# Twenty-eight stores of a hybrid encoder layer, moved from the SP queue to ScalarE's queue

## The chip, the cores and the metric

The kernel runs on one core of one Trainium2 chip, as one program in one launch. The metric is the device time of an execution in microseconds (us), the median of several runs. TensorE (PE) multiplies matrices, VectorE (DVE), ScalarE (ACT) and GpSimd (POOL) work on elements, and SyncE (SP) only issues transfers. Each engine takes its own instructions strictly in order and waits for others by semaphores.

## The reference

One layer of a bidirectional encoder, for 512 tokens of width 1024, in float32. Cut to what matters:

```python
u = x @ w_in                                  # z | x,B,C | dt | q | k | v | gate logits
y_ssd = ssd_branch(z, xbc, dt_f, dt_b, ...) @ w_proj_ssd      # chunked scan in both directions
y_att = attention_branch(q, k, v) @ w_proj_attn               # dilated windows, 12 heads
gates = sigmoid(gate_logits + b_gate)
mix = (gates[:, :, 0] * y_ssd + gates[:, :, 1] * y_att) @ w_out
h = layer_norm(alpha * x + mix, ln1_g, ln1_b)
f = square(relu(h @ w_up)) @ w_down
out = layer_norm(alpha * h + f, ln2_g, ln2_b)
```

## The kernel before

Each product is made of three matmuls (helper `mm3`, L124 to L126): both factors are split into a high and a low part in a reduced float32 format. For a weight tile, `Stream` loads the raw tile on SP (`wraw`, L86, three buffers), ScalarE casts the high part (`wh`, L103) and VectorE subtracts to get the low part (`wl`, L104); `wh` and `wl` have two buffers each, so wh72 takes the buffer of wh70 and wraw80 that of wraw77. Numbers count the weight tiles: tiles 60 to 75 are the gate tiles g0 to g15, tiles 76 and on belong to the projection of the scan's output (`ps_pa`).

The program runs in stages: v and dt first, then the state space scan in four groups of eight heads each, mixed on TensorE with the 6 q, 6 k and 16 gate tiles and the other column tiles of `w_in`; then attention, mixed with the projection; then the merge, the first norm and the two matrix products of the channel part. Within a group the heads come in pairs. For each head ScalarE and VectorE build a 128x512 matrix in pieces of 128x128: `U` from two broadcast rows `bc` (L439 on ScalarE, L441 on VectorE, exponential L442), `G1` and `G2` (L444 and L445 on ScalarE), their sum (L446) and product with `U` (L447) on VectorE. When both heads of pair j are there, TensorE makes `ps_y` of that pair (L348); then come `yt` (L350 on VectorE, L351 on GpSimd), `y` (L352 on VectorE) and its square `sq` (L354 on ScalarE). Group 3 has pairs 12 to 15, that is heads 24 to 31. Later `yh` (L542, ScalarE) and `yl` (L543, VectorE) split y0 to y15 for the projection.

The q, k and gate tiles of the middle stage leave the chip's on-chip memory: `evict` reads the sum from PSUM on ScalarE into a staging tile of 256 KB (tag `stage`, two buffers) and stores it to DRAM. The q and k tiles are loaded again by `load_qk` in attention (L558 and L559), the gates in `proj_a` and `proj_b` (L755 and L763).

TensorE's order is written out by hand (`manual_schedule`). On VectorE, ScalarE and SP a scheduler orders the instructions by its own estimates, so it also decides between which rows a store stands. The loads of attention follow on SP behind the raw weight load wraw80, which needs the slot that wl77 frees.

Of the kernel before, what the change touches and what calls it, by code (L numbers as in the profile page):

```python
# [43 lines left out]
def hybrid_layer_kernel(ctx: ExitStack, tc: tile.TileContext, t: dict, out: bass.AP):  # L44
    nc = tc.nc
    act, dve, pool, pe, dma = nc.scalar, nc.vector, nc.gpsimd, nc.tensor, nc.sync
# [15 lines left out]
    dr_qk = dram.tile([12, P, S], F32, name="dr_qk")  # L62
    dr_v = dram.tile([S, 768], F32, name="dr_v")
    dr_gate = dram.tile([16, P, S], F32, name="dr_gate")
# [203 lines left out]
    def conv_silu(ps, ci, dst):  # L268

        w = lambda k: vec[:, V_CW + ci * 5 + k:V_CW + ci * 5 + k + 1]  # L270
        acc = sp.tile([P, S], F32, name=f"acc{ci}", tag="acc", bufs=2)
        act.activation(acc, ps, AF.Identity, bias=vec[:, V_CB + ci:V_CB + ci + 1], scale=w(2))
        for k, (o0, o1, i0, i1) in ((0, (2, S, 0, S - 2)), (1, (1, S, 0, S - 1)), (3, (0, S - 1, 1, S)), (4, (0, S - 2, 2, S))):
            dve.scalar_tensor_tensor(acc[:, o0:o1], ps[:, i0:i1], w(k), acc[:, o0:o1], op0=ALU.mult, op1=ALU.add)
        act.activation(dst, acc, AF.Tanh)
        dve.scalar_tensor_tensor(dst, dst, 1.0, acc, op0=ALU.add, op1=ALU.mult)

    def tile_task(kind, j):

        wh, wl = ws.get()  # L280
        ps = ps_tile("mm", f"ps_{kind}{j}", 3)
        for k in range(0, KT, 2):
            last_mm[0] = mm3(ps, [(wh[:, q * P:(q + 1) * P], wl[:, q * P:(q + 1) * P]) for q in (k, k + 1)], xs_hl[k:k + 2], k == 0, k == KT - 2)
            if k < KT - 2:
                yield QT
        evict(kind, j, ps)
        yield QT

    def evict(kind, j, ps):
        if kind == "x":  # L290
            dst = sp.tile([P, S], F32, name=f"x{j}", tag="x", bufs=8)
            conv_silu(ps, j, dst)
            fm["x", j] = dst
        elif kind in "BC":
            dst = sp.tile([P, S], F32, name=f"{kind}{j}", tag=kind, bufs=2)
            conv_silu(ps, (16 if kind == "B" else 20) + j, dst)
            fm[kind, j] = dst
        elif kind == "z":
            th = ys[j]
            act.activation(th, ps, AF.Tanh, scale=0.5)  # L300
            dve.scalar_tensor_tensor(th, th, 1.0, ps, op0=ALU.add, op1=ALU.mult)
        elif kind == "g":
            st = xp.tile([P, S], F32, name=f"g{j}", tag="stage", bufs=2)
            act.activation(st, ps, AF.Tanh, scale=0.5, bias=vec[:, V_BG + j:V_BG + j + 1])
            dma.dma_start(dr_gate[j], st)
        else:
            st = xp.tile([P, S], F32, name=f"{kind}{j}", tag="stage", bufs=2)
            sc = 0.125 if kind == "q" else 1.0
            if j < 2:
                act.activation(st, ps, AF.Copy, scale=sc)  # L310
            else:
                act.activation(st.rearrange("p (r i) -> p i r", r=4), ps.rearrange("p (i r) -> p i r", r=4), AF.Copy, scale=sc)
            dma.dma_start(dr_qk[{"q": 0, "k": 6}[kind] + j], st)

    last_mm = [None]

# [718 lines left out]
```

## Time and profile before

| | |
|---|---|
| three runs | 1036.61, 1035.73 and 1035.19 us, median 1035.73 |
| the profiled execution | 1036.7 us, its span in the profile 1034.9 us |
| mean granted clock of TensorE | 0.995 |
| median from issue to landing, 256 KB store of a gate tile | 2.0 us |
| the same, 256 KB load of a q or k tile | 4.3 and 4.7 us |
| the same, 512 KB raw weight tile of `w_in` | 3.5 us |
| all DMA | 140.42 MB, 136 GB/s over the span |

The span is the time from the first to the last recorded instruction on the core; starts in the timeline count from its beginning. A busy TensorE says little of its pace, since matmuls overlap; what counts is where it waits, and whether the waiting one is the engine on whose end the whole ends. All transfers before the change go through one queue, SP's.

### The profile page before, as it was taken

What the parts mean: (1) busy time and instruction counts of PE and PEld (TensorE: products, weight loads), DVE (VectorE), ACT (ScalarE), POOL (GpSimd) and SP (SyncE); (2) the same over time, 40 slices, a digit from 0 to 9 for tenths busy, and PEclk for the clock granted to TensorE, in tenths of its full rate; (3) what the DMA queues carried; (4) which work ended last, traced back from release to release, by engine and by line L of the source; (5) the groups of instructions that cost most, each with busy time, mean ns of one, the idle gap of its engine ahead of it and who ended that gap; (6) DMA issues with size and microseconds to landing.
All of it is one profiled execution on the core that took longest, in us unless ns stands there. A gap on an engine that the chain in (4) does not pass through costs nothing.

```text
span 1034.9 us, 13695 instructions
## 1 busy us (share of the span) xinstructions
PE 1018.9 (98%) x5169; PEld 843.6 (82%) x5169; DVE 650.1 (63%) x1009; ACT 511.1 (49%) x1009; POOL 73.5 (7%) x66
## 2 busy tenths in 40 slices
PE   9999999999999999999899999999999999999997
PEld 7888888888888888888678787898888888888886
DVE  4296978689979897874886276844442334443346
ACT  4444877478758865984564334224332213433120
POOL 0000101221131022121000000000000000000000
PEclk9999999999999999999899999999999999999999
DMA  6444355425542654564753168312332333333322
GB/s 235 148 161 130 122 184 173 143 87 176 179 150 94 193 178 148 180 197 148 249 164 86 58 188 311 101 42 62 102 91 92 102 102 98 88 101 102 96 88 81
DMA packets 48305, 140.42 MB, mean 136 GB/s; under 512 B 6512, under 2 KB 7280, under 8 KB 47984
## 3 DMA queue, kind: packets, MB, share of 16 engines
q1 hardware_dynamic: 48240, 139.56, 43.0%
q8 instruction: 40, 0.66, 0.3%
q14 instruction: 25, 0.20, 0.1%
HBM read 128.25 MB, written 11.30 MB: 135 GB/s over the span
## 4 chain that ended last, share of the span: by engine, by line
PE 89%; DMA 4%; DVE 4%; ACT 2%; issue 1%; SPq 0%; DVEq 0%; ACTq 0%
PE ps_u L125 6%; PE ps_u L124 6%; PE ps_d L124 6%; PE ps_u L126 6%; PE ps_d L125 6%; PE ps_d L126 6%; PE ps_z L124 3%; PE ps_z L125 3%; PE ps_z L126 3%; PE ps_g L124 3%; PE ps_g L125 3%; PE ps_g L126 3%; PE ps_x L124 2%; PE ps_x L126 2%; PE ps_x L125 2%; PE ps_pa L124 2%
## 5 line engine op out<-in xcount | busy, mean ns | idle before, releaser
L104 DVE TENSOR_TENSOR wl<-wraw,wh 128x1024 fp32r<-128x1024 f32 (+1 forms) x166 | 202.5, 1223 | 240.7 <-ACT wh L103 233.7
L103 ACT CAST wh<-wraw 128x1024 fp32r<-128x1024 f32 (+1 forms) x166 | 172.2, 1040 | 261.0 <-PE ps_d L126 108.6
L125 PE MATMUL ps_u<-htl,wh 128*128 128x512 f32 (+1 forms) x288 | 105.1, 366 | 0.3 <-DVE htl L877 0.3
L126 PE MATMUL ps_u<-hth,wl 128*128 128x512 f32 (+1 forms) x288 | 105.1, 365 | 0.0
L124 PE MATMUL ps_u<-hth,wh 128*128 128x512 f32 (+1 forms) x288 | 104.5, 366 | 0.3 <-ACT hth L876 0.2
L125 PE MATMUL ps_d<-wl,fh 128*128 128x512 f32 (+1 forms) x272 | 102.5, 377 | 0.0
L124 PE MATMUL ps_d<-wh,fh 128*128 128x512 f32 (+1 forms) x272 | 102.4, 377 | 0.0
L126 PE MATMUL ps_d<-wh,fl 128*128 128x512 f32 (+1 forms) x272 | 102.4, 377 | 0.0
L125 PEld LDWEIGHTS ps_u<-htl,wh 128*128 128x128 f32 x288 | 54.3, 189 | 9.2 <-DVE htl L877 0.5
L124 PEld LDWEIGHTS ps_u<-hth,wh 128*128 128x128 f32 x288 | 53.9, 189 | 9.5 <-ACT hth L876 0.7
L126 PEld LDWEIGHTS ps_u<-hth,wl 128*128 128x128 f32 x288 | 54.3, 189 | 8.8
L126 PEld LDWEIGHTS ps_d<-wh,fl 128*128 128x128 f32 x272 | 51.2, 188 | 9.5
L124 PEld LDWEIGHTS ps_d<-wh,fh 128*128 128x128 f32 x272 | 51.2, 188 | 9.4
L125 PEld LDWEIGHTS ps_d<-wl,fh 128*128 128x128 f32 x272 | 51.2, 188 | 9.3
L124 PE MATMUL ps_pa<-yh,wh 128*128 128x512 f32 x128 | 53.1, 415 | 0.0
L441 DVE SCALAR_TENSOR_TENSOR U<-bc,acr,U 128x128 f32<-128x128 f32 x128 | 47.9, 409 | 6.1 <-ACT U L439 5.9
L124 PE MATMUL ps_g<-xh,wh 128*128 128x512 f32 x128 | 51.4, 402 | 0.0
L125 PE MATMUL ps_pa<-yl,wh 128*128 128x512 f32 x128 | 50.9, 397 | 0.2 <-DVE yl L543 0.2
L124 PE MATMUL ps_x<-xh,wh 128*128 128x512 f32 x128 | 50.9, 398 | 0.0
L124 PE MATMUL ps_z<-xh,wh 128*128 128x512 f32 x128 | 50.9, 398 | 0.0
L126 PE MATMUL ps_pa<-yh,wl 128*128 128x512 f32 x128 | 50.7, 396 | 0.0
L126 PE MATMUL ps_x<-xh,wl 128*128 128x512 f32 x128 | 49.9, 390 | 0.0
(257 smaller groups left out, 2194.7 us busy)
## 6 DMA issues: line engine op xcount, KB each, us to landing
wraw<-in_w_in_dram SPq DMA_DIRECT2D x68, 512.0 KB, 3.5
bc<-dr_acr SPq DMA_DIRECT2D x32, 512.0 KB, 4.3
wraw<-in_w_up_dram SPq DMA_DIRECT2D x32, 512.0 KB, 3.6
wraw<-in_w_dn_dram SPq DMA_DIRECT2D x32, 512.0 KB, 3.6
be<-dr_ear SPq DMA_DIRECT2D x32, 256.0 KB, 4.4
wraw<-in_w_ps_dram SPq DMA_DIRECT2D x16, 512.0 KB, 3.7
dr_gate<-g SPq DMA_DIRECT2D x16, 256.0 KB, 2.0
wraw<-in_w_out_dram SPq DMA_DIRECT2D x8, 512.0 KB, 4.8
```

The lines of the kernel that those rows point to most:

```text
L103: act.copy(h[:, :width], r[:, :width])
L104: dve.tensor_sub(l[:, :width], r[:, :width], f32(h[:, :width]))
L124: pe.matmul(ps, lh, rh, start=(first and i == 0), stop=False)
L125: pe.matmul(ps, lh, rl, start=False, stop=False)
L126: ins = pe.matmul(ps, ll, rh, start=False, stop=(last and i == n - 1))
L441: dve.scalar_tensor_tensor(U[:, ch(c)], bcs[0][:, hh, ch(c)], acr[:, c, h:h + 1], U[:, ch(c)], op0=ALU.subtract, op1=ALU.min)
```

## The change

The two stores in `evict` are issued by `act` (ScalarE) where `dma` (SP) issued them. Nothing else in the source is touched.

```diff
         elif kind == "g":
...
             act.activation(st, ps, AF.Tanh, scale=0.5, bias=vec[:, V_BG + j:V_BG + j + 1])
-            dma.dma_start(dr_gate[j], st)
+            act.dma_start(dr_gate[j], st)
         else:
...
-            dma.dma_start(dr_qk[{"q": 0, "k": 6}[kind] + j], st)
+            act.dma_start(dr_qk[{"q": 0, "k": 6}[kind] + j], st)
```

The order of TensorE and of GpSimd stays the same. SP loses its 28 stores, ScalarE gets them, and the scheduler orders ScalarE, VectorE and SP anew. In the rows below a name carries the number of its head, pair or tile first (G1_31 is head 31, y14 pair 14, wh72 weight tile 72), then a buffer number; x2 counts equal rows.

ScalarE around the cast of weight tile 72, in the last group of the scan, before:

```order
L442 ACTIVATE U31_4529<-U31_4529 128x512
L445 ACTIVATE G2_31_4531<-cb1_3_3773,tok_164 128x128
L444 ACTIVATE G1_31_4530<-cb0_3_3771,tok_164 128x128
L445 ACTIVATE G2_31_4531<-cb1_3_3773,tok_164 128x128
L444 ACTIVATE G1_31_4530<-cb0_3_3771,tok_164 128x128
L445 ACTIVATE G2_31_4531<-cb1_3_3773,tok_164 128x128
L103 CAST wh72_4553<-wraw72_4366 128x1024
L304 ACTIVATE g10_4510<-ps_g10_4485,vec_64 128x512
L354 ACTIVATE sq14_4526<-y14_97 128x512
```

ScalarE at the same place with the change:

```order
L103 CAST wh72_4553<-wraw72_4366 128x1024
L304 ACTIVATE g10_4510<-ps_g10_4485,vec_64 128x512
L439 ACTIVATE U31_4529<-bc3_3_1_4440,acr_165 128x128
L305 DMA dr_gate_73<-g10_4510 128x512
L439 ACTIVATE U31_4529<-bc3_3_1_4440,acr_165 128x128
L444 ACTIVATE G1_31_4530<-cb0_3_3771,tok_164 128x128
L445 ACTIVATE G2_31_4531<-cb1_3_3773,tok_164 128x128
L444 ACTIVATE G1_31_4530<-cb0_3_3771,tok_164 128x128
L445 ACTIVATE G2_31_4531<-cb1_3_3773,tok_164 128x128
L442 ACTIVATE U31_4529<-U31_4529 128x512
L354 ACTIVATE sq14_4526<-y14_97 128x512
L444 ACTIVATE G1_31_4530<-cb0_3_3771,tok_164 128x128
```

All of head 31's pieces moved behind wh72, and the last four of them (one shown) behind sq14; the store of g10 stands one row behind its activation.

ScalarE between the casts wh71 and wh72 with the change (the work that stands ahead of wh72 there):

```order
L103 CAST wh71_4481<-wraw71_4291 128x1024
L304 ACTIVATE g9_4435<-ps_g9_4372,vec_64 128x512
L445 ACTIVATE G2_30_4459<-cb1_3_3773,tok_164 128x128
L305 DMA dr_gate_73<-g9_4435 128x512
L439 ACTIVATE U30_4457<-bc3_3_1_4440,acr_165 128x128 x4
L444 ACTIVATE G1_30_4458<-cb0_3_3771,tok_164 128x128
L445 ACTIVATE G2_30_4459<-cb1_3_3773,tok_164 128x128
L442 ACTIVATE U30_4457<-U30_4457 128x512
```

Four more pieces of G1_30 and G2_30 and two of U31 follow before wh72; before the change head 31 stood here.

VectorE around the low part of weight tile 72, before:

```order
L446 TENSOR_TENSOR G1_31_4530<-G1_31_4530,G2_31_4531 128x512
L447 TENSOR_TENSOR G1_31_4530<-G1_31_4530,U31_4529 128x512
L104 TENSOR_TENSOR wl72_4554<-wraw72_4366,wh72_4553 128x1024
L350 SCALAR_TENSOR_TENSOR yt14_4522<-x14_3490,vec_64,ps_y14_4513 128x512
L352 TENSOR_TENSOR y14_97<-y14_97,yt14_4522 128x512
```

VectorE at the same place with the change:

```order
L104 TENSOR_TENSOR wl72_4554<-wraw72_4366,wh72_4553 128x1024
L350 SCALAR_TENSOR_TENSOR yt14_4522<-x14_3490,vec_64,ps_y14_4513 128x512
L441 SCALAR_TENSOR_TENSOR U31_4529<-bc3_3_0_4438,acr_165,U31_4529 128x128 x3
L352 TENSOR_TENSOR y14_97<-y14_97,yt14_4522 128x512
L446 TENSOR_TENSOR G1_31_4530<-G1_31_4530,G2_31_4531 128x512
L447 TENSOR_TENSOR G1_31_4530<-G1_31_4530,U31_4529 128x512
```

Head 31's sum and product moved from ahead of wl72 to behind y14. TensorE's `ps_y15`, which needs them, stands where it stood, between weight tiles 71 and 72.

VectorE at the end of the scan, before:

```order
L543 TENSOR_TENSOR yl2_4790<-y2_85,yh2_4770 128x512
L543 TENSOR_TENSOR yl3_4793<-y3_86,yh3_4771 128x512
L104 TENSOR_TENSOR wl77_4870<-wraw77_4863,wh77_4869 128x1024
L543 TENSOR_TENSOR yl4_4796<-y4_87,yh4_4772 128x512
L543 TENSOR_TENSOR yl5_4799<-y5_88,yh5_4773 128x512
```

The same with the change:

```order
L543 TENSOR_TENSOR yl2_4790<-y2_85,yh2_4770 128x512
L543 TENSOR_TENSOR yl3_4793<-y3_86,yh3_4771 128x512
L543 TENSOR_TENSOR yl4_4796<-y4_87,yh4_4772 128x512
L104 TENSOR_TENSOR wl77_4870<-wraw77_4863,wh77_4869 128x1024
L543 TENSOR_TENSOR yl5_4799<-y5_88,yh5_4773 128x512
```

yl4 moved ahead of wl77. SP at this place, before:

```order
L86 DMA wraw79_4867<-in_w_ps_dram 128x1024
L305 DMA dr_gate_73<-g14_4704 128x512
L755 DMA ga2_5308<-dr_gate_73 128x512
L305 DMA dr_gate_73<-g15_4741 128x512
L86 DMA wraw80_4924<-in_w_ps_dram 128x1024
L558 DMA q0_4841<-dr_qk_71 128x512
L559 DMA k0_4842<-dr_qk_71 128x512
```

And with the change:

```order
L86 DMA wraw79_4867<-in_w_ps_dram 128x1024
L755 DMA ga2_5308<-dr_gate_73 128x512
L86 DMA wraw80_4924<-in_w_ps_dram 128x1024
L558 DMA q0_4841<-dr_qk_71 128x512
L559 DMA k0_4842<-dr_qk_71 128x512
```

The two gate stores are gone from SP, and the loads keep their order.

## The prediction

> **What bounds the kernel now.** I read the page first, then the kernel cut into stretches, then who waits for whom on TensorE and on the SP queue, and last the timeline at two places.
>
> ```profile
> span 1034.9 us, 13695 instructions
> ...
> PE 1018.9 (98%) x5169; PEld 843.6 (82%) x5169; DVE 650.1 (63%) x1009; ACT 511.1 (49%) x1009; POOL 73.5 (7%) x66
> ```
>
> TensorE is busy for 1018.9 of 1034.9 us, so everything that waits costs at most 16.0 us. The stretches below (from:to, length, then busy time of PE, PEld, DVE, ACT, POOL, then granted clock, DMA share, GB/s) say where these lie around the stores, which are issued from 124.8 to 495.7 us.
>
> ```profile
> 120.00:388.00 268.00, 267.68 (x1411) 221.62 (x1410) 229.22 (x380) 195.13 (x436) 47.51 (x39) 1.00 0.50 158
> 388.00:474.00 86.00, 86.00 (x479) 71.38 (x478) 67.31 (x108) 64.99 (x151) 18.02 (x16) 1.00 0.54 170
> 474.00:500.00 26.00, 24.39 (x114) 19.66 (x113) 14.65 (x20) 17.87 (x28) 2.58 (x2) 1.00 0.59 181
> 500.00:530.00 30.00, 27.23 (x140) 20.49 (x141) 22.64 (x67) 14.23 (x50) 0.00 (x0) 0.89 0.70 223
> ```
>
> From 120 to 474 us TensorE idles 0.32 us in all. A store that leaves SP cannot speed up what does not wait. Only the start of attention has something to win: 1.61 + 2.77 us idle, and a clock of 0.89. The waits of TensorE and of SP (in total, times, longest):
>
> ```profile
> PE ps_s L591 <- DMA k<-dr_qk: 4.2, 1, 4.2
> ...
> SPq L86 <- DVE wl L104: 565.0, 141, 28.1
> ...
> SPq L305 <- ACT g L304: 40.1, 12, 5.7
> ```
>
> SP stands 40.1 us behind gate tiles that ScalarE has not finished, but 565.0 us behind VectorE for the slot of a raw weight tile, which stays. The one stall of TensorE is on the first k load of attention.
>
> **The change part by part.** *Issue cost.* 28 stores go from SP to ScalarE (durations in ns, least/median/most):
>
> ```profile
> L305 SPq DMA_DIRECT2D dr_gate<-g x16: 319/320/462, 391.2 to 495.7; - x16
> ...
> L313 SPq DMA_DIRECT2D dr_qk<-q x6: 319/330/545, 124.8 to 225.9; - x6
> ```
>
> SP saves 28 x 0.32 = 9 us, worth nothing since TensorE does not wait there. No row shows a store issued by ScalarE. The order puts it mostly one row behind its activation, so the row between can cover it: from below 0 us, from above SP's median of 0.32 to 0.33 (I bound it by 0.46, the slowest gate store). Queued behind it on ScalarE are the casts (wh) of the next weight tile. Their cover is the lead of the split weights over TensorE; the tightest I found is this one, where wl ends at 448.17 and the tile starts at 448.77:
>
> ```profile
> 446.94 1.23 DVE L104 TENSOR_TENSOR wl<-wraw,wh 128x1024 fp32r<-128x1024 f32 x1 [0.23 <-ACT wh L103]
> 448.77 0.39 PE L124 MATMUL ps_g<-xh,wh 128*128 128x512 f32 x1
> ```
>
> One issue of 0.46 fits in these 0.6 us; I take 0 for this term and up to 1 us in the range. The data itself goes to the same place and in the same amount: 0.
>
> *Term 1, the last head of group 3.* The order shows more than the diff. Before, ScalarE has made all pieces of head 31 ahead of the cast wh72, and VectorE its last product (L447) ahead of wl72. Afterwards wh72 and wl72 stand ahead of them, and so does all of pair 14's tail: yt14, y14 and sq14. Only then can TensorE start ps_y15, at 469.03 today:
>
> ```profile
> 418.36 0.39 ACT L444 ACTIVATE G<-cb,tok 128x128 f32<-128x128 f32 x1
> 418.65 0.39 ACT L445 ACTIVATE G<-cb,tok 128x128 f32<-128x128 f32 x1
> ...
> 456.71 0.48 PE L124 MATMUL ps_g<-xh,wh 128*128 128x512 f32 x1
> 459.86 1.03 ACT L103 CAST wh<-wraw 128x1024 fp32r<-128x1024 f32 x1
> 460.80 0.68 ACT L304 ACTIVATE g<-ps_g,vec 128x512 f32<-128x512 f32 x1
> 461.38 0.68 ACT L439 ACTIVATE U<-bc,acr 128x128 f32<-128x128 f32 x2
> 462.03 0.39 PE L126 MATMUL ps_g<-xh,wl 128*128 128x512 f32 x1
> 464.98 1.04 ACT L103 CAST wh<-wraw 128x1024 fp32r<-128x1024 f32 x1
> 465.11 0.69 DVE L446 TENSOR_TENSOR G<-G,G 128x512 f32<-128x512 f32 x1 [1.17 <-ACT G L445]
> 465.83 0.69 DVE L447 TENSOR_TENSOR G<-G,U 128x512 f32<-128x512 f32 x1
> 466.44 1.22 DVE L104 TENSOR_TENSOR wl<-wraw,wh 128x1024 fp32r<-128x1024 f32 x1
> 467.58 0.74 DVE L350 SCALAR_TENSOR_TENSOR yt<-x,vec,ps_y 128x512 f32<-128x512 f32 x1
> 468.40 1.28 POOL L351 TENSOR_TENSOR yt<-yt,be 128x512 f32<-128x512 f32 x1 [3.58 <-DVE yt L350]
> 469.03 1.09 PE L348 MATMUL ps_y<-G,xt 128*64 128x128 f32 x16
> 469.71 0.69 DVE L352 TENSOR_TENSOR y<-y,yt 128x512 f32<-128x512 f32 x1 [1.39 <-POOL yt L351]
> 470.43 0.63 ACT L354 ACTIVATE sq<-y 128x512 f32<-128x512 f32 x1 [3.83 <-DVE y L352]
> 470.97 1.04 ACT L103 CAST wh<-wraw 128x1024 fp32r<-128x1024 f32 x1
> 472.04 1.48 DVE L104 TENSOR_TENSOR wl<-wraw,wh 128x1024 fp32r<-128x1024 f32 x1 [1.64 <-ACT wh L103]
> ```
>
> Columns are start, length, engine and line. By starts: a piece of a head takes 0.29 (418.36 to 418.65), a cast 0.94 (459.86 to 460.80), a gate 0.58 (to 461.38), and an activation of 128x512 without a bias 0.54 (470.43 to 470.97), which I use for the exponential. wh71 cannot start before tile g9 lets its buffer go, at 456.71. From wh71 to wh72 the new order has 13 pieces, one exponential, one cast, one gate: 3.8 + 0.54 + 0.94 + 0.58 = 5.9, so wh72 comes at 462.6 plus an issue of 0 to 0.46, just behind the release of its own buffer (462.03 + 0.39 = 462.42). From there wl72 follows by 1.07 (470.97 to 472.04) and yt14 by another 1.14 (466.44 to 467.58): 464.8 to 465.2. Then along the chain: 0.82 to POOL, 1.31 to y14, 0.72 to sq14, 0.54 for it, four pieces 3 x 0.29 + 0.39 = 1.26, 0.03 and 0.72 for L446, 0.69 for L447, 6.1 in all. Head 31 is ready at 470.9 to 471.3 instead of 466.5, and TensorE waits 1.9 to 2.3 us where it waits nothing now. If ScalarE runs as late as today (wh72 at 464.98), it is 464.98 + 2.21 + 6.1 = 473.3: 4.3 us. I take 2.3, since the walk gives it with the store counted. Nothing behind makes up for it: TensorE's order is fixed and full up to 474.
>
> *Term 2, the start of attention.* VectorE now makes yl4 ahead of wl77. wl77 frees the slot for the raw weight load that stands ahead of q0 and k0 on SP:
>
> ```profile
> 492.29 3.07 DVE L543 TENSOR_TENSOR yl<-y,yh 128x512 fp32r<-128x512 f32 x4
> 495.27 1.22 DVE L104 TENSOR_TENSOR wl<-wraw,wh 128x1024 fp32r<-128x1024 f32 x1
> 496.52 0.33 SPq L86 DMA_DIRECT2D wraw<-in_w_ps_dram  x1
> 497.38 0.42 SPq L559 DMA_DIRECT2D k<-dr_qk  x1
> 498.21 0.40 PE L126 MATMUL ps_pa<-yh,wl 128*128 128x512 f32 x1
> 502.77 1.86 PE L591 MATMUL ps_s<-k,q 64*128 64x192 f32 x8 [4.16 <-DMA k<-dr_qk]
> 505.15 0.63 PE L125 MATMUL ps_pa<-yl,wh 128*128 128x512 f32 x1
> 508.56 0.63 PE L124 MATMUL ps_pa<-yh,wh 128*128 128x512 f32 x1
> ```
>
> The raw load was issued when wl77 ended (496.49), not when the g15 store let SP go. One more yl is 3.07 / 4 = 0.77 us, so k0 lands 0.8 later at most; a little less with that store out of SP's queue. I take 0.7, range 0 to 0.8. The matmuls behind the gap run slow whether it is 4.2 or 4.9 us long: the nine from 505.15 to 508.56 take 0.63 each where this form took 0.39 at 462.03, 9 x 0.24 = 2.2 us that stay.
>
> Sum: 2.3 + 0.7 + 0 = 3.0 us. The profiled execution took 1036.7 (span 1034.9 and 1.8 around it), which gives 1039.7. That execution is 1.0 above the median of the three runs, 1035.73, so the forecast for a median is **1038.7 us**.
>
> **The rivals.** *No change* (within 0.2%, 2.1 us, about what a measurement of this kernel can tell from none). ScalarE gets ahead of today's times: its loads bc came late, and with SP free they may come sooner:
>
> ```profile
> 441.43 1.28 ACT L439 ACTIVATE U<-bc,acr 128x128 f32<-128x128 f32 x4 [2.27 <-DMA bc<-dr_acr]
> ```
>
> For it speaks also that ScalarE was busy for only 65.0 of the 86.0 us up to 474. Against: even the earliest wh72 leaves 1.9. It would take head 31 ready 1 us sooner than the walk, or term 2 at nothing: 1036 to 1037.5.
>
> *Faster.* The loads of q0 and k0, no longer behind stores, land before TensorE is through at 498.6; then 4.2 us of waiting and the 2.2 of slow matmuls go, less term 1: 1035.7 - 6.4 + 2.3 = 1031.6. [...] Against it stand the rows: the load in front waited for VectorE. It decides once k0 is issued 4.2 us sooner, at 493.2, which wl77 at 496.5 forbids.
>
> *Slower still.* The wait at ps_y15 grows until the clock falls there too. Rows here bound that point only loosely: 4.16 us of waiting were followed by slow matmuls. With 4.3 for term 1, another 2.2 of slow matmuls, 0.8 and 1 for issue cost it is 8.3 us: 1044.0. [...]
>
> **How the numbers follow.** Chances: the forecast 0.57 (its own range 1037.6 to 1040.5), no change 0.27, faster 0.06, the cold clock 0.10. The range takes in no change below, 1035.3, and above the upper ends without the cold clock: 1035.7 + 4.3 + 0.8 + 1 = 1041.8. Slower by over 0.2% (above 1037.8): 0.10 + nearly all of 0.57, 0.65; within 0.29; faster 0.06.
>
> **What would show it.** Right: a wait of TensorE on L447 (or on G) of about 2 us at ps_y15, absent now; sq14 between the pieces of head 31 with ScalarE idle before it; wl77 after five yl, and the wait for k near 4.9; the 120 to 456 us stretch as full as now; SP's waits behind L304 gone. Wrong: no wait at ps_y15, because wh72 and yt14 run ahead of the walk, or store issues that hold ScalarE for far more than 0.46 us, which would show as weights (wh or wl) that TensorE waits for, many times and early.

## The result and the profile after

The changed kernel takes **1045.76 us** (median of six runs, 1040.58 to 1049.32), the kernel before 1036.69 in the same comparison: ratio 1.009, interval 1.0072 to 1.0109. It is slower, by 9.1 us where 3.0 were forecast (1038.7), and outside the range (1035.3 to 1041.8). The profiled execution took 1046.14 us, 9.4 more than the one of before; its span grew by 9.5. Of the runs compared below, one each of e15, of e16 and of the kernel before beside them lay far out (3343.89, 5188.33 and 1133.97 us); their ratios are of the other runs.

The head of the page of the changed kernel:

```profile
span 1044.4 us, 13677 instructions
...
PE 1021.1 (98%) x5169; PEld 844.7 (81%) x5169; DVE 648.8 (62%) x1009; ACT 512.8 (49%) x1009; POOL 76.0 (7%) x66
```

TensorE idles 1044.4 - 1021.1 = 23.3 us, where it idled 16.0: 7.3 of the 9.5 us. The other 2.2 are busy time, 1021.1 against 1018.9, for the same 5169 matmuls: some ran slower. The stretches of the changed kernel, in the columns used before (the last one is moved by 10 us, since attention now starts 11 us later):

```profile
120.00:388.00 268.00, 266.95 (x1407) 221.01 (x1406) 228.21 (x379) 195.73 (x436) 49.42 (x39) 1.00 0.49 157
388.00:474.00 86.00, 82.15 (x451) 67.93 (x449) 63.17 (x103) 62.24 (x143) 17.26 (x15) 0.99 0.54 165
474.00:500.00 26.00, 21.78 (x103) 18.16 (x104) 7.38 (x10) 10.37 (x16) 3.83 (x3) 0.82 0.38 122
510.00:540.00 30.00, 26.35 (x143) 19.66 (x142) 24.41 (x69) 15.70 (x53) 0.00 (x0) 0.94 0.75 245
```

Up to 388 us it lost 0.7 us. From 388 to 500 it now idles 3.85 + 4.22 us, where it idled 0 + 1.61, and the granted clock there fell to 0.82. TensorE's waits say on what:

```profile
PE ps_y L348 <- ACT g L304: 7.1, 1, 7.1
PE ps_s L591 <- DMA k<-dr_qk: 3.6, 1, 3.6
...
PE ps_y L348 <- DVE G L447: 0.9, 1, 0.9
...
PE ps_xt L389 <- ACT xt L391: 0.7, 1, 0.7
```

Both waits at `ps_y` are one stop, at ps_y15. The timeline of TensorE, VectorE and ScalarE there (start, length, engine, line; idle time before and its end in brackets):

```profile
449.45 1.28 ACT L439 ACTIVATE U<-bc,acr 128x128 f32<-128x128 f32 x4 [4.15 <-DMA bc<-dr_acr]
...
460.69 1.03 ACT L103 CAST wh<-wraw 128x1024 fp32r<-128x1024 f32 x1
...
465.40 1.28 ACT L439 ACTIVATE U<-bc,acr 128x128 f32<-128x128 f32 x4 [2.80 <-DMA bc<-dr_acr]
...
469.45 1.03 ACT L103 CAST wh<-wraw 128x1024 fp32r<-128x1024 f32 x1
...
470.69 0.40 PE L348 MATMUL ps_y<-G,xt 128*64 128x128 f32 x2 [0.95 <-DVE G L447]
...
470.97 0.39 ACT L439 ACTIVATE U<-bc,acr 128x128 f32<-128x128 f32 x1
471.09 0.33 ACTq L305 DMA_DIRECT2D dr_gate<-g  x1
471.47 0.40 ACT L439 ACTIVATE U<-bc,acr 128x128 f32<-128x128 f32 x1
...
471.65 0.74 DVE L350 SCALAR_TENSOR_TENSOR yt<-x,vec,ps_y 128x512 f32<-128x512 f32 x1
472.31 1.88 DVE L441 SCALAR_TENSOR_TENSOR U<-bc,acr,U 128x128 f32<-128x128 f32 x3
...
474.22 0.63 ACT L442 ACTIVATE U<-U 128x512 f32<-128x512 f32 x1 [1.19 <-DVE U L441]
474.83 0.63 ACT L354 ACTIVATE sq<-y 128x512 f32<-128x512 f32 x1
...
477.38 0.69 DVE L447 TENSOR_TENSOR G<-G,U 128x512 f32<-128x512 f32 x1
478.22 1.94 PE L348 MATMUL ps_y<-G,xt 128*64 128x128 f32 x14 [7.13 <-ACT g L304]
...
480.68 0.63 PE L125 MATMUL ps_g<-xl,wh 128*128 128x512 f32 x1
```

Two matmuls of ps_y15 run on head 30 at 470.69; the others wait for head 31's product, which ends at 477.38 + 0.69 = 478.07 (the releaser named, the gate activation, had ended long before). Behind the stop the 128x512 matmuls take 0.63 us instead of 0.39 and start 0.43 apart instead of 0.23: about half the pace. The reader also sees why head 31 is late: ScalarE stood 4.15 and 2.80 us for loads `bc`, so wh71 came at 460.69 and wh72 at 469.45; and its exponential waited for pieces that VectorE makes behind yt14. (Not all of head 31 moved behind wh72: as the listing between wh71 and wh72 says, two of its pieces of `U` still stand ahead of it.) A store issue on ScalarE takes 0.33 us, and the piece behind it starts 0.50 after the one ahead (470.97 to 471.47) instead of 0.29: 0.21 us each.

The loads `bc` on SP, each time with the row of ScalarE that lets go of the first buffer (the end of head 27's `U`), of before and then of the changed kernel:

```profile
431.53 2.44 ACT L439 ACTIVATE U<-bc,acr 128x128 f32<-128x128 f32 x8
...
433.99 2.63 SPq L458 DMA_DIRECT2D bc<-dr_acr  x2
...
448.69 0.87 SPq L458 DMA_DIRECT2D bc<-dr_acr  x2
```

```profile
438.19 0.39 ACT L439 ACTIVATE U<-bc,acr 128x128 f32<-128x128 f32 x1
...
438.61 0.33 SPq L458 DMA_DIRECT2D bc<-dr_acr  x1
439.04 0.40 SPq L86 DMA_DIRECT2D wraw<-in_w_in_dram  x1
439.53 0.40 SPq L458 DMA_DIRECT2D bc<-dr_acr  x1
...
455.43 0.33 SPq L458 DMA_DIRECT2D bc<-dr_acr  x1
456.21 0.33 SPq L86 DMA_DIRECT2D wraw<-in_w_in_dram  x1
457.39 0.33 SPq L458 DMA_DIRECT2D bc<-dr_acr  x1
```

Pair 14's first load goes out as soon as that `U` is through, at 438.61 behind 438.19 + 0.39 = 438.58, before at 433.99 behind 433.97: the new order has put the end of head 27's `U` behind a cast (436.68) that stood behind it before. Pair 15's second load is issued at 457.39 instead of some 449, and raw weight loads (wraw71, wraw73) now stand ahead of the second bc of a pair. The loads also land later, the one of 439.53 after 9.9 us (before: 5.1 for the same load):

```profile
bc<-dr_acr SPq DMA_DIRECT2D x1, 512.0 KB, 9.9
```

### The profile page after: what moved, and what is told of

Same layout as the page of the kernel before. It is cut to its first block, busy times and chain, and to the rows that moved or that the text cites. A ratio compares the mean times of both kernels' runs of the same rounds, so it can differ in the third digit from the quotient of the medians.

```text
span 1044.4 us, 13677 instructions
## 1 busy us (share of the span) xinstructions
PE 1021.1 (98%) x5169; PEld 844.7 (81%) x5169; DVE 648.8 (62%) x1009; ACT 512.8 (49%) x1009; POOL 76.0 (7%) x66
## 4 chain that ended last, share of the span: by engine, by line
PE 80%; DVE 7%; DMA 6%; ACT 3%; issue 2%; POOL 1%; SPq 0%; DVEq 0%; POOLq 0%; ACTq 0%
PE ps_u L125 6%; PE ps_u L124 6%; PE ps_u L126 6%; PE ps_d L124 6%; PE ps_d L126 6%; PE ps_d L125 6%; PE ps_z L124 2%; PE ps_z L125 2%; PE ps_z L126 2%; DVE wl L104 2%; PE ps_pa L124 2%; PE ps_g L124 2%; PE ps_g L125 2%; PE ps_g L126 2%; PE ps_pa L125 2%
## 5 line engine op out<-in xcount | busy, mean ns | idle before, releaser
L125 PE MATMUL ps_g<-xl,wh 128*128 128x512 f32 x128 | 50.4, 394 | 0.0
L126 PE MATMUL ps_g<-xh,wl 128*128 128x512 f32 x128 | 50.4, 394 | 0.0
```

Source lines behind the costliest of these rows:

```text
L125: pe.matmul(ps, lh, rl, start=False, stop=False)
L126: ins = pe.matmul(ps, ll, rh, start=False, stop=(last and i == n - 1))
```

## The experiments

The theories, in the order in which they were formed: **A**, the order of SP's loads (wraw71 and wraw73 ahead of bc) costs; **B**, the order of ScalarE and VectorE (the listing of the changed kernel shows the heads of group 3 about one head later against the casts: behind wh69 stands head 28, where it was head 29); **C**, the hold of ScalarE by each issue; **D**, what SP's queue does once the stores are gone. Ratios are to the kernel before, run beside each.

| run | stores on | ps_y15 waits, us | ratio (interval) |
|---|---|---|---|
| e1 | GpSimd | 0 | 0.9996 (0.9986 to 1.0005) |
| e2 | SP, loads in the new order | 0 | 0.9999 (0.9989 to 1.0009) |
| e3 | ScalarE, loads in the old order | 4.9 | 1.0062 (1.0046 to 1.0079) |
| e4 | ScalarE, ps_y15 later | 0 | 1.0017 (1.0007 to 1.0028) |
| e5 | ScalarE: gates only | 5.1 | 1.0079 (1.0060 to 1.0099) |
| e6 | ScalarE: q and k only | 0 | 1.0016 (1.0007 to 1.0026) |
| e7 | SP, heads late | 3.3 | 1.0052 (1.0032 to 1.0071) |
| e8 | ScalarE, all heads early | 0 | 1.0164 (1.0142 to 1.0187) |
| e9 | ScalarE, heads of group 3 earlier | 2.2 | 1.0047 (1.0035 to 1.0060) |
| e10 | SP, k0 ahead of wraw80 | 0 | 0.9968 (0.9955 to 0.9980) |
| e11 | GpSimd, k0 ahead of wraw80 | 0 | 0.9965 (0.9953 to 0.9978) |
| e12 | as e9, k0 ahead of wraw80 | 2.1 | 1.0021 (1.0011 to 1.0031) |
| e13 | ScalarE, heads and gates earlier | 0 | 1.0066 (1.0049 to 1.0084) |
| e14 | as e13, k0 ahead of wraw80 | 0 | 1.0020 (1.0006 to 1.0035) |
| e15 | SP, 1 filler in a new tile | 0 | 1.0063 (1.0042 to 1.0083) |
| e16 | SP, 3 fillers in a new tile | 0 | 1.0073 (1.0051 to 1.0095) |
| e17 | SP, 3 fillers, no new tile | 0 | 0.9997 (0.9984 to 1.0011) |
| e18 | as e9, loads in the old order | 2.3 | 1.0042 (1.0028 to 1.0056) |

**e1.** The diff is `pool.dma_start` where the change has `act.dma_start`, in both places.

> All 28 stores are issued by GpSimd instead of ScalarE. They leave SP as in the changed kernel, but the program keeps the order of before: 3 of 949 instructions of ScalarE stand elsewhere (99 in the changed kernel), and on SP the loads bc of pairs 14 and 15 stand ahead of the raw weight loads wraw71 and wraw73 as before. Theory A (the cost is the new order of SP's loads, wraw71 and wraw73 ahead of the second bc of pairs 14 and 15): no wait at ps_y15, 1034 to 1038 us. Theory B (the cost is the new order of ScalarE and VectorE, head 31 behind wh72, wl72 and sq14): the same, 1034 to 1038. Theory C (issuing a store from ScalarE holds it): the same. Theory D (stores that no longer pass SP's queue release its loads in bursts, and these collide): a wait of several us at ps_y15 here too, 1041 to 1047.

No wait and no difference that can be told. Leaving SP's queue costs nothing here (ratio 0.9996), so D falls; it also brings nothing by itself.

**e2 and e3: the loads' order, put in and taken out.** e2 is the kernel before with

```diff
             for d in range(2):
+                swap = g == 3 and pr > 1 and d == 1
+                if swap:
+                    ws.load(67 + 2 * pr)
...
-                dma.dma_start(b2, ...)
+                with tc.issue_after(ws.last.ins) if swap else ExitStack():
+                    dma.dma_start(b2, ...)
```

> The kernel before, stores on SP, with one thing of the changed kernel: in pairs 14 and 15 the second bc load is issued behind the raw weight load (wraw71, wraw73), as there. Head 31 still stands ahead of wh72 on ScalarE. Theory A: bc of pair 15 is issued 3 to 8 us later than before, TensorE waits 3 to 8 us at ps_y15, 1039 to 1046 us. Theories B and C: no wait at ps_y15, 1035 to 1038.

No wait, so the loads' order alone does not make one. But the test is weak: the scheduler had also moved the pieces G of heads 30 and 31 ahead of their U, which lets ScalarE bear a later load; the new order of loads under ScalarE's order of before was not run. e3 is the changed kernel with

```diff
+                with tc.issue_after(bcl[i]) if i in bcl else ExitStack():
                     dma.dma_start(r[:, :width], ap)
...
+                with tc.high_priority(1000) if (g == 3 and pr > 1) else ExitStack():
+                    ld = dma.dma_start(b2, ...)
+                bcl[67 + 2 * pr if (g == 3 and d and pr > 1) else -1] = ld.ins
```

> The changed kernel, stores on ScalarE in the same order there (head 31 behind wh72 and sq14), with the second bc load of pairs 14 and 15 ahead of wraw71 and wraw73 again. Theory A: bc lands some 4 and 9 us sooner, the waits of ScalarE for it shrink from 4.2 and 2.8 to under 1 us, the wait at ps_y15 falls from 7.1 to 1.9 to 4.3 us (what the order of ScalarE is worth by the prediction's walk), no slow clock there, 1037 to 1041 us. Theory B (order of ScalarE and VectorE alone) and C (issue on ScalarE): the wait stays at 7 us, 1044 to 1047.

TensorE's wait at ps_y15 in e3:

```profile
PE ps_y L350 <- ACT g L306: 4.9, 1, 4.9
```

That is less than the 8.1 of the changed kernel (0.95 + 7.13), and no more than the 5.1 of e5, which has the loads in the new order. ScalarE waits for no bc here, but VectorE stands 3.12 us for the load `be` (until 449.58) and ScalarE 2.79 us for VectorE (until 455.23): with bc put first, another load came late. So the order of SP's loads does not decide, and most of the wait stays without it, above the 1.9 to 4.3 of the walk.

**e4.** The changed kernel with the last `y_out` behind tile g12 in the tail:

```diff
-        y_out(*late[0])
         for n, (k, j) in enumerate(mix[3][rest:]):
...
             if n == 0:
+                y_out(*late[0])
                 nrm = norm(3)
```

> The changed kernel with the last y_out traced behind tile g12 in the tail, so TensorE has 5.5 us of matmuls between g11 and ps_y15 (its order is fixed by the code). If the wait at ps_y15 and the slow clock behind it are the whole loss: the wait falls from 7.1 to 1.6 to 2.6 us, no slow clock there, 1036 to 1039.5 us. If store issues on ScalarE cost something all along: 1 us or more above that.

The wait vanishes and with it all but 0.17% of the loss, though the stores stay on ScalarE and its order there as in the changed kernel. So nearly all of the loss is this one stop and the slow matmuls behind it. That not even the expected 1.6 to 2.6 us are left has a reason of its own, and it tells most about the change. ScalarE and then VectorE in e4:

```profile
446.11 1.28 ACT L439 ACTIVATE U<-bc,acr 128x128 f32<-128x128 f32 x4 [0.60 <-DMA bc<-dr_acr]
...
463.75 1.03 ACT L103 CAST wh<-wraw 128x1024 fp32r<-128x1024 f32 x1
...
471.82 0.69 DVE L447 TENSOR_TENSOR G<-G,U 128x512 f32<-128x512 f32 x1
```

From 400 us to head 31's product both engines run through the same rows as in the changed kernel, but the loads bc land sooner, and so everything behind them is sooner. The same holds for e5 below, so that one order was traced three times:

| | pair 14's second bc lands after | ScalarE waits for bc, pairs 14 and 15 | wh71 | wh72 | head 31's product ends |
|---|---|---|---|---|---|
| the walk of the prediction | | none | 456.71 | 462.6 | 470.9 |
| e4 | 6.8 | 0.60 and 0 | 457.39 | 463.75 | 472.51 |
| e5 | 8.4 | 2.21 and 0.99 | 458.31 | 465.25 | 474.52 |
| the changed kernel | 9.9 | 4.15 and 2.80 | 460.69 | 469.45 | 478.07 |

TensorE stood ready at 469.6 in e5. With e4's product it would have waited some 3 us there (an estimate from these two traces); so of the 8.1 us some 3 belong to the order of ScalarE and VectorE, and some 5 to the late landing of loads (9.9 us where e4 has 6.8) that this order issues close together, three of 512 KB from 438.61 to 439.53 in the changed kernel.

**e5 and e6: the change in two halves.** Each puts one of the two `act.dma_start` back to `dma.dma_start`.

> Only the 16 gate stores on ScalarE, the 12 of q and k on SP as before. In group 3 ScalarE and VectorE have the order of the changed kernel: head 28 behind the cast wh69, where before it is head 29, and sq14 ahead of the last pieces of head 31. Theory B (order of ScalarE and VectorE: the heads of group 3 stand about one head later against the casts): the wait at ps_y15 is there, 5 to 8 us, 1042 to 1047 us. Theory C (holding of ScalarE by each store issue): 16 of 28 stores, and all of those near ps_y15, so the same wait. If the q and k stores matter: several us less.

> Only the 12 stores of q and k on ScalarE, the gates on SP. From head 24 on ScalarE, VectorE and SP have the order of before. Theory B: no wait at ps_y15, 1034.5 to 1038 us. If an issue on ScalarE costs what SP's does (0.33 us) and is not hidden: 12 x 0.33 = 4 us, 1040.

The gates alone bring nearly all of it. The twelve q and k stores cost 0.16%, 1.6 us (interval 0.7 to 2.7), in which the profile shows 0.8 us at ps_xt, as in the changed kernel (0.7); what the rest is, is not shown.

**e7: the order without the stores.** The kernel before with

```diff
+                with tc.issue_after(casts[69]) if j == 14 else ExitStack():
                     ms.append(head(pr, 0, bcs))
...
+            with tc.issue_after(yts[14]) if j == 15 else ExitStack():
                 ms.append(head(pr, 1, bcs))
```

where `casts[i]` is the cast of weight tile i and `yts[j]` the instruction that makes yt of pair j.

> The kernel before, all stores on SP, with two added edges of order that put head 28 behind the cast wh69 on ScalarE, and head 31's work on VectorE behind yt14, as in the changed kernel. No store on ScalarE. Theory B: a wait of 4 to 8 us at ps_y15 and the slow clock behind it, 1040 to 1047 us. Theory C (issue on ScalarE) and theory D (what SP's queue does without the stores): no wait, 1035 to 1038.

TensorE's timeline in e7 (the gap again behind two matmuls of ps_y15):

```profile
472.54 1.34 PE L350 MATMUL ps_y<-G,xt 128*64 128x128 f32 x14 [3.29 <-DVE G L449]
473.81 0.79 PE L126 MATMUL ps_g<-xh,wh 128*128 128x512 f32 x1
474.40 0.63 PE L127 MATMUL ps_g<-xl,wh 128*128 128x512 f32 x1
```

No store is on ScalarE, and the stop and the slow clock are there (granted 0.95 from 474 to 500 us, matmuls of 0.63 us), if with 3.3 us less than the 4 to 8 expected; it fits the 3 us that e4 leaves to the order. The edge is a little stronger than the change (all four pieces of head 31 behind yt14, not three), and wh72 came in time, at 464.55, so it shows what this part of the order costs, not the whole 7.1.

**e8, e9, e13: the order put back with the stores on ScalarE.** All three edit the two calls of `head`; e13 the gates too.

```diff
+                with tc.high_priority(130):
                     ms.append(head(pr, 0, bcs))
...
+            with tc.high_priority(130):
                 ms.append(head(pr, 1, bcs))
```

That is e8; e9 has 70 and only in group 3, e13 has 115 there and 100 around the gate activation and its store.

> The changed kernel, all 28 stores on ScalarE, with the heads given a higher priority, so that ScalarE makes head 29 ahead of wh70, head 30 ahead of wh71 and head 31 ahead of wh72 and sq14, about as before. Theory B: the wait at ps_y15 under 1 us, no slow clock there, 1034 to 1038 us. Theory C: the wait stays above 4 us, 1042 or more.

> The changed kernel, all 28 stores on ScalarE; only the heads of group 3 get a higher priority (70), so that ScalarE makes head 31 ahead of sq14 and VectorE all its pieces ahead of yt14, as before. Groups 0 to 2 are left as in the changed kernel. Theory B (order): the wait at ps_y15 is 0 to 1 us, no slow clock there, 1034.5 to 1038.5 us. Theory C (issue on ScalarE): the wait stays above 4 us, 1042 or more.

> The changed kernel, all 28 stores on ScalarE; in group 3 the heads get priority 115 and the gate activations with their stores 100, so that all pieces of head 31 stand ahead of wh72 on ScalarE and its four pieces on VectorE ahead of yt14, nearer to before than in the run that left 2.2 us of wait. Theory B (order): no wait above 0.5 us at ps_y15, no slow clock there, 1035 to 1038.5 us. Theory C (issue on ScalarE): the wait stays at 2 us or more with the slow clock, 1040 or more.

Three misses in time, each instructive. In e8 the wait at ps_y15 is gone, but TensorE stops earlier, for VectorE's work at L274 (8.2 us at ps_k) and for a gate tile's buffer (2.2). In e13 TensorE waits for casts instead:

```profile
PE ps_g L124 <- ACT wh L103: 3.2, 1, 3.2
...
PE ps_g L126 <- DVE wl L104: 1.0, 1, 1.0
```

So it reaches ps_y15 only at 477.45, when head 31's product, still behind y14 on VectorE, has ended at 475.45: no wait there, but no order of before either. e9 leaves 2.2 us at ps_y15; there too VectorE makes head 31's sum and product behind y14 (470.64 and 471.36, y14 at 470.03). Moving heads forward pushes something else back; none of the priorities tried gave the order of before.

**e18 and e17: what is left to the issue itself.** e18 joins e9's edit and e3's.

> All 28 stores on ScalarE; heads of group 3 with priority 70 (which alone left a wait of 2.2 us) and the second bc load of pairs 14 and 15 ahead of wraw71 and wraw73 (which alone left 4.9). Theory B with the loads as its second half: ScalarE waits under 1 us for bc in these pairs, head 31 is ready ahead of its place, no wait above 0.5 us at ps_y15, no slow clock there, 1035 to 1038.5 us. Theory C (issue on ScalarE): 2 us or more of wait, 1039.5 or more.

The 2.3 us stayed, which is what theory C had forecast and not B. But ScalarE still waits 3.05 us for a bc, and head 31's product (470.99) still stands behind y14 (469.33), so the run does not part the two. e15, e16 and e17 ask it the other way: the kernel before, with ScalarE held behind every gate activation. e15 (one) and e16 (three) write to a new tile of 64 bytes a partition, e17 (three) to free columns of one that is there.

```diff
             act.activation(st, ps, AF.Tanh, scale=0.5, bias=vec[:, V_BG + j:V_BG + j + 1])
+            for i in range(3):
+                act.copy(epsv[:, 8 + i:9 + i], st[:, i:i + 1])
             dma.dma_start(dr_gate[j], st)
```

> The kernel before, all stores on SP, with a one-column activation (128x1) on ScalarE behind each of the 16 gate activations, where the changed kernel has its store: it holds ScalarE for about 0.2 us, as a store does there (417.98 to 418.49, where two such pieces follow each other in 0.29 us). It leaves the heads ahead of the casts: head 31 ahead of wh72, bc ahead of wraw71 and wraw73, as before. Theory C (ScalarE held 0.2 us per store): a wait of 2 us or more at ps_y15, 1039 to 1046 us. Theory B (order): no wait, 1035 to 1037.5.

> The same with three such activations behind each gate, some 0.6 us, three times what a store takes. Theory C: a longer wait than with one, 1042 us or more. Theory B: 0 to 1 us of wait, 1035 to 1038.5.

> The kernel before with three one-column activations behind each gate on ScalarE, writing into unused columns of a tile that is there already, so that no other tile moves in SBUF (the run before with them in a tile of its own had no wait at ps_y15, but slower matmuls of ps_pa and ps_u from 540 us on). By the timeline of the run with one, each takes 0.08 us, so three take about what a store issue takes (0.21). Theory C (the hold of ScalarE): a wait of 2 us or more at ps_y15, 1039 us or more. Theory B (order): no wait there, 1034.5 to 1037.5. If the slower matmuls come from the place of the tiles in SBUF, ps_u is back at 366 ns a matmul (371 in that run).

None waits at ps_y15. In e17 the three hold ScalarE for 0.27 us a gate (the piece behind starts at 440.79), more than a store's 0.21:

```profile
440.52 0.36 ACT L306 COPY epsv<-g 128x1 f32<-128x1 f32 x3
440.79 0.40 ACT L447 ACTIVATE G<-cb,tok 128x128 f32<-128x128 f32 x1
```

With head 31 ahead of wh72, as before, the hold is absorbed: head 31's product ends at 467.86, 1.3 us later than before, and TensorE comes to it at 470.31. The changed kernel's own trace says the same of its order: behind each of the five stores from 438.32 to 471.09 ScalarE stands idle ahead of the next cast, for 0.68, 4.15, 0.60, 2.80 and 1.19 us, waiting for VectorE or a load, and 0.21 us fits into each. So C falls as the cause of the stop. The 0.6 and 0.7% of e15 and e16, outside their ranges, came from elsewhere (last section). Not tried is a kernel with the stores on ScalarE in exactly the order of before; that the stores are harmless in it is argued, not shown.

**e10, e11, e12, e14: the start of attention.** One edge, so that wraw80 is issued behind k0 instead of ahead of q0 (`kq` collects the loads of k):

```diff
+                with tc.issue_after(kq[0]) if i == 80 else ExitStack():
                     dma.dma_start(r[:, :width], ap)
...
-            dma.dma_start(qk[n][1], dr_qk[6 + n])
+            kq.append(dma.dma_start(qk[n][1], dr_qk[6 + n]).ins)
```

> The kernel before, stores on SP, with one added edge of order: the raw weight load wraw80 is issued behind k0 instead of ahead of q0. k0 can then be issued behind the store of g15, about 0.9 us sooner, and shares the DMA engines with 512 KB less. [...]

> The stores on GpSimd's queue (order of before, no cost by itself) and wraw80 behind k0. Nothing is left on SP between the load ga2 (491 us) and q0, so k0 can be issued at 491 to 492 us if its buffer is free, and lands before TensorE is through at 498.2: no wait for k, no slow clock, 1029.5 to 1032 us. This is what leaving SP can bring at most. If the buffer comes free only near 496: as the kernel with k0 first and stores on SP, 1030 to 1035.

> Stores on ScalarE, heads of group 3 with priority 70, and wraw80 behind k0. Theory B: no wait at ps_y15 and none or under 2 us for k: 1030 to 1034 us, faster than before. Theory C: over 1040.

> The same with wraw80 issued behind k0. Theory B: no wait at ps_y15, and the wait for k at 0 to 1.5 us without slow clock: 1030.5 to 1034 us, faster than before. Theory C: as the run without this edge less 3 to 5 us, 1036 or more.

e10 (stores on SP) and e11 (stores on GpSimd) beat both kernels, by 0.3%, near 1032 us. TensorE and SP in e10, then SP in e11:

```profile
496.43 0.45 SPq L561 DMA_DIRECT2D k<-dr_qk  x1
...
500.00 1.03 PE L593 MATMUL ps_s<-k,q 64*128 64x192 f32 x8 [1.47 <-DMA k<-dr_qk]
...
501.29 0.40 PE L127 MATMUL ps_pa<-yl,wh 128*128 128x512 f32 x1
```

```profile
491.26 0.43 SPq L561 DMA_DIRECT2D k<-dr_qk  x1
```

In e10 the wait falls from 4.2 to 1.5 us and no slow matmuls follow (0.40 us at 501.29, granted clock 1.00 from 500 to 540 us): k0 is issued 0.95 us sooner and lands 3.4 us after its issue instead of 5.3. In e11 k0 is issued 6 us sooner than before, and that wait is gone. But the gain is that of moving the load in front: e10 has it with the stores on SP, and between 0.9968 and 0.9965 no further gain of leaving SP can be told. e12 and e14 miss their ranges: the wait for k0 is gone there too (they are 2.5 and 4.5 us faster than e9 and e13), but the losses of e9 and e13 stay.

## Why the prediction was right and wrong

**Right: sign and place, and the order as one half of the mechanism.** The stretch to 388 us stayed full but for 0.7 us; TensorE waits at ps_y15 for head 31's last product, behind wh72, yt14 and with sq14 between the pieces (e4, e5 and e7 confirm it); wl77 follows five yl; and SP's waits behind L304 are gone without any gain (e1).

**Wrong: the size of term 1**, 2.3 taken and 4.3 as its upper end, against 0.95 + 7.13. The step that failed is the start of the walk: wh71 was put at the release of its buffer, 456.71, and ScalarE was let run from there without a gap. Its upper end lets ScalarE be as late as before, no later. Measured against the walk: wh71 at 460.69, 4.0 later; from wh71 to wh72 8.76 us instead of 5.9, of which 2.80 are the wait for bc; from wh72 to head 31's product 478.07 - 469.45 = 8.6 instead of 2.2 + 6.1 = 8.3. Together 7.2 us, which is what head 31 is later than 470.9. The walk began two casts ahead of the place and took ScalarE's lateness at its start for zero, though the same order that it read had shifted every head of the group, so that ScalarE released bc late (438.58 for 433.97) and got the next one late. The prediction named these loads only as something that might come sooner; they came later. Where they landed sooner, in e4, the same walk is off by 1.6 us only, and inside its upper end of 473.3. The 8.3 us of its last part came out near by a path that it left out: between yt14 and y14 VectorE makes three pieces of `U` (472.31), for which the exponential, and behind it sq14, waits; that cost 0.3 us.

**Wrong: the price of a wait.** The step was that a wait of 2.3 us is spared the slow clock, and the sum adds 0 for it. No run shows that term: the trace of before has no wait near 2.3 (its 4.16 was followed by slow matmuls), and the runs show slow matmuls in its place. TensorE's rows at ps_y15 in e9, where 2.15 were followed by them (two small matmuls ran just ahead of the wait):

```profile
472.20 1.25 PE L348 MATMUL ps_y<-G,xt 128*64 128x128 f32 x14 [2.15 <-DVE G L447]
...
473.97 0.63 PE L125 MATMUL ps_g<-xl,wh 128*128 128x512 f32 x1
```

So even the forecast's own 2.3 us should have carried slow matmuls, in e9 six that start 0.43 us apart, some 1.2 us; behind the 2.27 of e18, the 2.15 of e12 and the 3.29 of e7 stood seven, two and five of 0.63 us. (The 2.2 us that the prediction counts behind k0 are also too many: it compared durations, which overlap. By starts, 0.43 for 0.23, the nine cost 1.8.)

**Wrong, and small: term 2.** The wait for k became 3.6 us, not 4.9: wl77 came behind a fifth yl as forecast, but k0 landed 4.0 us after its issue, where it took 5.3 before and the term let it stay. Over the runs without the k0 edge the wait lay between 3.0 (e17) and 4.9 (e3), so a profile cannot tell 0.7. **Not refuted: the issue term**, 0 to 1 us. The hold is 0.21 us of ScalarE each, and it found room; the 1.6 us of e6 and the 0.17% of e4 lie above the 1 us, with a cause that stays open.

**The rivals.** "Slower still" is what happened, by its own mechanism: waits of 8.1 and 2.2 of slow matmuls, less what other waits gave back. It had a chance of 0.10 and 1044.0 us, near the 1045.76 measured, and the range was cut below it. That it came so near is in part luck: it had 4.3 us for the stop where 8.1 came, and made up for it with 1 us for issues and 0.8 for k0, which did not come. "Faster" did not come. e11 shows what it needed, k0 by 493.2: there it goes out at 491.3, and the wait and the slow matmuls behind it are gone; but the load in front had to be moved for that, and with it moved the stores may stay on SP (e10).

## What to carry to other kernels

Where a scheduler fills in the order, moving an issue to another engine is an edit of the order: list it for the whole stage, find where the shift begins, and walk from there with every load that waits for a buffer of that chain, since a walk that starts late takes the lateness at its start for zero. Give such a load a range for its landing: here one order was worth some 3 us or 8, as the loads landed. Price a new wait of the bounding engine with the slow pace that the runs show behind one (here two to nine matmuls of 0.63 us for 0.39, behind waits of 2.15 us and more). To make a load come sooner, look at what stands in front of it in its queue and what that waits for: moving that one gained 0.3% here, and clearing the rest of the queue gave nothing that can be told, without that move (0.9996) or with it (0.9965 for 0.9968).

## What the runs showed of the hardware

Behind twelve gaps in TensorE's work stood slow pace, two to nine 128x512 matmuls of 0.63 us each time: 2.15 us (e9 and e12), 2.27 (e18), 3.28 (e1), 3.29 (e7), 3.62 (e9), 3.65 and 7.13 (the changed kernel), 3.80 (e4), 3.87 (e6), 4.16 (the kernel before) and 4.89 (e3). Shorter gaps went either way, so that the gap alone does not decide. The 1.47 us of e10 were followed by none, and so were 1.81 and, one matmul later, 0.76 us in e6, and 0.73 and 0.77 us in the kernel before (0.40 at 646.23); 0.92 and 0.75 us in e11 were followed by slow pace, 0.63 us at 641.08. First e11, then e6:

```profile
639.80 0.51 PE L127 MATMUL ps_o<-wl,mixh 128*128 128x512 f32 x1 [0.75 <-DVE wl L105]
...
641.08 0.63 PE L126 MATMUL ps_o<-wh,mixh 128*128 128x512 f32 x1
```

```profile
645.06 0.50 PE L124 MATMUL ps_o<-wh,mixh 128*128 128x512 f32 x1 [1.81 <-ACT wh L103]
...
646.88 0.39 PE L124 MATMUL ps_o<-wh,mixh 128*128 128x512 f32 x1
```

A tile of 64 bytes more per partition went with a loss of 0.6 and 0.7% (e15, e16): in both the matmul groups of `ps_u` take 370 to 371 ns, and 365 to 366 in the kernel before and in e17, which has e16's three copies but no new tile. First e15, then e17:

```profile
L126 PE MATMUL ps_u<-htl,wh 128*128 128x512 f32 (+1 forms) x288 | 106.6, 371 | 0.3 <-DVE htl L879 0.3
```

```profile
L125 PE MATMUL ps_u<-htl,wh 128*128 128x512 f32 (+1 forms) x288 | 105.1, 366 | 0.3 <-DVE htl L879 0.3
```

TensorE waits there no longer than in the others (0.3 us). The sources of e16 and e17 differ only in where the copies write, so the place of the operands in SBUF is the author's estimate of the reason; it was not shown, and why it should matter stays open.

The same 512 KB load, issued at the same place of the same order, landed after 6.8, 8.4 and 9.9 us (e4, e5, the changed kernel); in the order of before it landed after 5.1.
